# PSUM pools by stage, and a token shift evicted by ScalarE, in a hybrid decoder step

## The chip, the cores and the metric

The kernel runs on one core of one Trainium2 chip. The metric is the device time of one launch in microseconds. Each timed run executes the whole program; the profile is one further execution, recorded by the hardware profiler. TensorE's clock has two levels, 1.2 and 2.4 GHz; the profile gives the granted clock as a share of the upper one.

## The reference, cut to what matters

One layer of a decoder step. 1024 prompt tokens and 8 x 4 sample tokens (1056 in all, model width 1024) go through a norm, one wide projection `w_in`, two parallel branches (a causal convolution and an RWKV-7 recurrence) with gates, and a gated MLP. The change is about the token shift at the head of the recurrent branch:

```python
zr32 = zr.astype(f32)
prev = jnp.concatenate([shift_buf.astype(f32)[:, None, :], zr32[:, :-1]], axis=1)
new_shift = zr[:, -1]
xs = zr32 + (prev - zr32) * rw_mu.astype(f32)
```

So each shifted column is `(1 - mu) * z[t] + mu * z[t-1]`; the first token of the prompt has no predecessor (zero), and the first of each sample sequence has the one in `state_shift`. `zr` has 3360 columns: k, r and v with 1024 each, and 288 for the low-rank inputs of the decay, the in-context rate and the gate. The last row of each sequence is an output (`new_shift`).

## The kernel before

Activations stand with the channel on the partitions and the 1056 tokens along the free dimension, in three blocks of 352. Every projection is made in three fp32r matmuls per 128 channels (high by high, high by low, low by high part), so a tile of 128 output channels is 3 blocks x 8 x 3 = 72 matmuls. `wjob` (line 41) loads a weight tile, makes its high part on ScalarE (L48) and its low part on GpSimd (L49).

The stages are in order:

- `load_in` and `norm_in` (lines 207 to 249): load 9 token tiles and the parameters, transpose the parameters through PSUM (`turn`, copy out in L179), normalise, transpose the tokens (L244) and split them into `hH` and `hL` (L247, L248).
- `mixer_a`, the first mixer stage: four convolution tiles (`conv_proj`), three tiles of low-rank inputs (`lora_in`), and k, r and v of the first two of eight channel groups (`rkv_tile`). `weave` issues, between the matmuls of these tiles, the 30 taps of each convolution (L359, on VectorE) and the low-rank output projections (`lora_out`, evicted by ScalarE in L597, L602 and L609).
- `mixer_b`, the second mixer stage: the recurrence in 16 parts, each prepared (`prep`), staged (`stage`), combined and run through a serial chain of small matmuls (`chain`). `drive` issues these streams by a planned clock, and fills the time between with independent projections: the other 18 tiles of k, r, v, then 16 gate tiles (`gate`) and 8 tiles of the convolution's output (`conv_out`, L441). The streams share `T2N` = 12 SBUF tiles of 576 columns; a stream that finds too few of them free waits (`take`). `prep` takes eight, a group norm three, and one of the eight is held until the part's `stage` ends.
- `tail`: merge of the branches, `w_mix_out`, and the MLP.

The framework gives buffers out and orders each engine's queue before the run, by priorities that follow the order of issue; an instruction whose operands and buffer are free may come to stand in its engine's queue ahead of much that was issued before it. Each engine then works its queue strictly in that order.

PSUM has 8 banks. Both mixer stages and the norm stage share one set: 3 banks with tag `mm` for projections (pool `pm`), and in pool `pw` 2 banks with tag `w` and one each with tags `c`, `x` and `y`. The last three belong to `mixer_b` (`x` is the work tile of a triangular inverse in `stage`, filled in L1025 by a copy of `x0`, which GpSimd makes in L646).

Nine tiles of `mixer_a` and 18 of `mixer_b` go through `shifted`. There, per block, ScalarE writes `(1 - mu) * z` out of PSUM (L490); VectorE adds `mu * z` out of PSUM one column further (L486), adds the first column of the block from a copy `bcol` of the block before (L486 again), and copies the block's last column to `bcol` (L496). The last block also holds the samples: a 24-column add and an 8-column add with the loaded state (L486), and two copies of the last rows to `shcol` (L502, L503). The bank is free when VectorE is through with it.

Of the kernel before, what the change touches and what calls it, by code (L numbers as in the profile page):

```python
# [7 lines left out]
F32 = mybir.dt.float32  # L8
F32R = mybir.dt.float32r
I32 = mybir.dt.int32  # L10
AF = mybir.ActivationFunctionType
ALU = mybir.AluOpType
AX = mybir.AxisListType
PSUM = bass.MemoryType.PSUM
# [3 lines left out]
TP = 1024  # L18
NB = 3
BW = 352  # L20
# [5 lines left out]
NSH = 27  # L26
# [5 lines left out]
class Net:  # L32
# [68 lines left out]
    def build(self):  # L101
        with ExitStack() as es:
# [6 lines left out]
            with ExitStack() as e1:  # L109
                self.rp = self.pool(e1, "wraw", 1)  # L110
                with ExitStack() as e:
                    self.pm = self.pool(e1, "pm", 3, space=PSUM)
                    self.pw = self.pool(e1, "pw", 2, space=PSUM)
                    xs, w0 = self.load_in(e)
                    self.norm_in(e, xs)
                with ExitStack() as e:
                    self.t4 = self.pool(e, "t4", 8)
                    self.mixer_a(w0)
                self.mixer_b()
# [132 lines left out]
    def mixer_a(self, w0):  # L252
        nc, a = self.nc, self.a
# [3 lines left out]
        self.shT = self.cp.tile([128, NSH, 8], F32, name="shT")  # L257
        self.bcol = self.cp.tile([128, NSH, 2], F32, name="bcol")
        self.done = set()
# [221 lines left out]
    def shifted(self, w, j, out, m=128):  # L481

        nc = self.nc
        om, mu = self.omu[:m, j:j + 1], self.par["mu"][:m, j:j + 1]
        bc = self.bcol[:m, j]
        add = lambda o, i: nc.vector.scalar_tensor_tensor(out=o, in0=i, scalar=mu, in1=o, op0=ALU.mult, op1=ALU.add)  # L486

        def ev(b, s, ps):
            t0 = b * BW
            nc.scalar.activation(out=out[:m, s], in_=ps, func=AF.Copy, scale=om)  # L490
            n = min(TP - t0, BW)
            add(out[:m, t0 + 1:t0 + n], ps[:, 0:n - 1])
            if b:
                add(out[:m, t0:t0 + 1], bc[:, b - 1:b])
            if n == BW:
                nc.vector.tensor_copy(out=bc[:, b:b + 1], in_=ps[:, n - 1:n])  # L496
            else:
                x = out[:m, TP:T].rearrange("p (b t) -> p b t", t=4)
                z = ps[:, n:BW].rearrange("p (b t) -> p b t", t=4)
                add(x[:, :, 1:4], z[:, :, 0:3])  # L500
                add(x[:, :, 0], self.shT[:m, j])
                nc.vector.tensor_copy(out=self.shcol[:m, j, 0:1], in_=ps[:, n - 1:n])  # L502
                nc.vector.tensor_copy(out=self.shcol[:m, j, 1:9], in_=z[:, :, 3])  # L503
        yield from self.project_g(w, (self.hH, self.hL), 8, ev, m)
# [163 lines left out]

    T2N = 12

# [321 lines left out]
    def stage(self, n):  # L992

        nc = self.nc
        E, BK, PC, nin, v = self.pr[n]
        LQ = self.sg.tile([128, 8, 128], F32, tag="LQ", name="LQ")
        for g in range(2):
            c4 = slice(4 * g, 4 * g + 4)
            for x in range(2):
                p, q = slice(64 * x, 64 * x + 64), slice(64 - 64 * x, 128 - 64 * x)  # L1000
# [22 lines left out]
        X = self.pw.tile([128, 512], F32, tag="x", name="x", bufs=1)[:, 0:256].rearrange("p (a t) -> p a t", t=32)  # L1023
        tm = self.ln.tile([128, 8, 32], F32, tag="tm", name="tm")
        nc.vector.tensor_copy(out=X, in_=self.x0)  # L1025
        for s in range(31):
            a, m = s // 4 + 1, 31 - s
            nc.vector.tensor_tensor(out=tm[:, :a, :m], in0=L[:, s:s + 1, s + 1:32].to_broadcast([128, a, m]),  # L1028
                                    in1=X[:, :a, s:s + 1].to_broadcast([128, a, m]), op=ALU.mult)
            nc.vector.tensor_tensor(out=X[:, :a, s + 1:32], in0=X[:, :a, s + 1:32], in1=tm[:, :a, :m], op=ALU.add)  # L1030
        Xs = self.ln.tile([128, 8, 32], F32, tag="X", name="X")
# [650 lines left out]
```

## Time and profile before

| | us |
|---|---|
| median of three timed runs | 2560.39 |
| lowest and highest | 2559.02, 2569.00 |
| profiled execution | 2538.03 |
| its span, from the first to the last instruction | 2536.3 |
| busy in it: TensorE, VectorE, ScalarE, GpSimd | 2367.6, 1427.9, 918.7, 909.1 |
| mean granted clock of TensorE | 0.926 |

Times inside the profile are counted from the start of the span. The mixer's first stage runs from about 62 to 340 us, the second from 340 to 1470 us, the tail from there to the end; a window of the profile adds up what every engine did in such a stretch. PE is TensorE, PEld its weight loads, DVE VectorE, ACT ScalarE, POOL GpSimd, SP the engine that issues most DMAs; a q behind the name is the engine's queue. Matmuls overlap each other, so that a busy TensorE can still have gaps that the busy time does not show.

### The profile page before, as it was taken

Reading aid. Unit: us, or ns where it says so; the run is one execution under the profiler, and the core shown is the slowest. Engines: PE = TensorE matmul, PEld = TensorE weight load, DVE = VectorE, ACT = ScalarE, POOL = GpSimd, SP = SyncE. Lnnn points to the kernel's source line nnn. Section 1 sums busy time; section 2 is a strip of 40 time slices with the busy share of each in tenths; the row PEclk is TensorE's granted clock in tenths of the full one; section 3 lists DMA queues with packets and bytes.
Section 4 is the critical chain, followed back from the end, with each engine's and each line's share of the span. In section 5 each row is a group of like instructions: output and inputs, shape, how many; then the busy total and the mean of one; then the engine's idle time right before and its main releaser. Section 6 shows DMA issues by size and latency. Waiting matters only on the chain.

```text
span 2536.3 us, 41660 instructions
## 1 busy us (share of the span) xinstructions
PE 2367.6 (93%) x16094; PEld 2140.9 (84%) x16094; DVE 1427.9 (56%) x3588; ACT 918.7 (36%) x1748; POOL 909.1 (36%) x879
## 2 busy tenths in 40 slices
PE   5889989999788799999989999999999999999998
PEld 4878888777676677777777899999999999999998
DVE  5799955586646674555464434465444534445345
ACT  4133433354244354454434322333222222223125
POOL 3332253244324443443333243433323323323333
PEclk9899987898688698999779999999999999999999
DMA  3223443243233333533323854431111111111111
GB/s 104 56 60 130 171 149 89 81 121 93 78 89 79 93 107 83 140 98 94 94 64 96 273 178 131 128 128 44 44 47 48 44 51 44 47 48 41 54 46 75
DMA packets 307640, 230.64 MB, mean 91 GB/s; under 512 B 90492, under 2 KB 287123, under 8 KB 306921
## 3 DMA queue, kind: packets, MB, share of 16 engines
q1 hardware_dynamic: 307185, 227.80, 31.1%
q8 instruction: 127, 2.08, 0.4%
q14 instruction: 72, 0.59, 0.1%
q0 software_dynamic: 256, 0.17, 0.0%
HBM read 157.45 MB, written 70.45 MB: 90 GB/s over the span
## 4 chain that ended last, share of the span: by engine, by line
PE 66%; DVE 7%; DMA 7%; POOL 3%; issue 2%; ACT 1%; SPq 1%; POOLq 0%; DVEq 0%; ACTq 0%
PE mm L54 52%; PE w L54 7%; DMA L<-dL 4%; PE c L54 2%; PE y L54 2%; PE w L61 2%; DVE tm L1028 1%; DVE x L1030 1%; DVE t L961 1%; DMA ga<-d_ga 0%; POOL BK L982 0%; POOL wlo L49 0%; POOL LQ L1011 0%; DVE lnQ L666 0%; DVE v L486 0%
## 5 line engine op out<-in xcount | busy, mean ns | idle before, releaser
L54 PE MATMUL mm<-hH,whi 128*128 128x352 f32 (+1 forms) x2568 | 887.6, 346 | 27.0 <-DVE bcol L496 11.2
L54 PE MATMUL mm<-hL,whi 128*128 128x352 f32 (+1 forms) x2568 | 866.2, 337 | 0.2 <-DVE hL L248 0.2
L54 PE MATMUL mm<-hH,wlo 128*128 128x352 f32 (+1 forms) x2568 | 862.7, 336 | 0.0
L54 PEld LDWEIGHTS mm<-hH,whi 128*128 128x128 f32 (+1 forms) x2568 | 499.4, 194 | 55.9 <-issue 14.1
L54 PEld LDWEIGHTS mm<-hL,whi 128*128 128x128 f32 (+1 forms) x2568 | 500.9, 195 | 11.2 <-DVE hL L248 0.5
L54 PEld LDWEIGHTS mm<-hH,wlo 128*128 128x128 f32 (+1 forms) x2568 | 500.6, 195 | 8.7 <-issue 0.2
L49 POOL TENSOR_TENSOR wlo<-wraw,whi 128x1024 fp32r<-128x1024 f32 (+2 forms) x123 | 292.5, 2378 | 462.0 <-ACT whi L48 427.9
L48 ACT ACTIVATE whi<-wraw 128x1024 fp32r<-128x1024 f32 (+2 forms) x123 | 126.0, 1025 | 366.8 <-PE mm L54 270.1
L1544 DVE SCALAR_TENSOR_TENSOR c<-u,par,c 128x1024 f32<-128x1024 f32 x96 | 167.0, 1739 | 55.6 <-ACT c L1540 55.6
L359 DVE SCALAR_TENSOR_TENSOR sg<-cu,par,sg 128x1024 f32<-128x1024 f32 x120 | 185.1, 1550 | 3.4 <-ACT sg L357 1.7
L1514 DVE TENSOR_TENSOR u<-mm,rs 128x352 f32<-128x352 f32 x144 | 73.2, 509 | 186.5 <-PE mm L54 186.3
L54 PE MATMUL mm<-fH,whi 128*128 128x352 f32 x504 | 163.4, 324 | 0.0
L1569 DVE TENSOR_TENSOR acc<-mm,acc 128x352 f32<-128x352 f32 x168 | 86.8, 523 | 135.0 <-PE mm L54 135.0
L54 PE MATMUL mm<-fH,wlo 128*128 128x352 f32 x504 | 162.7, 323 | 0.0
L54 PE MATMUL mm<-fL,whi 128*128 128x352 f32 x504 | 162.7, 323 | 0.0
L1028 DVE TENSOR_TENSOR tm<-L,x 128x60 f32<-128x60 f32 (+24 forms) x496 | 99.4, 200 | 79.7 <-DMA L<-dL 72.5
L1030 DVE TENSOR_TENSOR x<-x,tm 128x60 f32<-128x60 f32 (+24 forms) x496 | 105.0, 212 | 7.0
L1525 POOL COPY lr<-u 128x2 f32<-128x2 f32 x48 | 9.0, 187 | 276.3 <-DVE u L1514 267.6
L54 PE MATMUL w<-E,BK 64*128 64x128 f32 x512 | 90.7, 337 | 8.8 <-DVE tm L1028 3.4
L1011 POOL TENSOR_SCALAR_AFFINE_SELECT LQ<-LQ 64x512 f32<-64x512 f32 x64 | 44.1, 690 | 148.3 <-ACT LQ L1007 146.8
L54 PEld LDWEIGHTS mm<-fH,whi 128*128 128x128 f32 x504 | 94.8, 188 | 0.5
L54 PEld LDWEIGHTS mm<-fH,wlo 128*128 128x128 f32 x504 | 95.0, 188 | 0.0
(379 smaller groups left out, 3971.2 us busy)
## 6 DMA issues: line engine op xcount, KB each, us to landing
wraw<-w_in SPq DMA_DIRECT2D x50, 512.0 KB
wraw<-w_up SPq DMA_DIRECT2D x48, 512.0 KB
wraw<-w_down SPq DMA_DIRECT2D x32, 384.0 KB
L<-dL SPq DMA_DIRECT2D x16, 512.0 KB
d_alr<-la SPq DMA_DIRECT2D x8, 528.0 KB
d_cum<-lc SPq DMA_DIRECT2D x8, 528.0 KB
d_gout<-lg SPq DMA_DIRECT2D x8, 528.0 KB
d_k<-k SPq DMA_DIRECT2D x8, 528.0 KB
```

What stands on the lines that cost most here:

```text
L48: nc.scalar.activation(out=hi[:, :nk, :m], in_=raw[:, :nk, :m], func=AF.Copy)
L49: (lo_eng or nc.gpsimd).tensor_tensor(out=lo[:, :nk, :m], in0=raw[:, :nk, :m], in1=hi[:, :nk, :m].bitcast(F32), op=ALU.subtract)
L54: self.nc.tensor.matmul(out, l, r, start=start, stop=stop)
L61: self.nc.tensor.transpose(out, x, ident)
L359: nc.vector.scalar_tensor_tensor(out=c[:, 0:TP], in0=u[:, t:t + TP], scalar=self.col("conv_w", t * 4 + i), in1=c[:, 0:TP], op0=ALU.mult, o ...
L961: nc.vector.scalar_tensor_tensor(out=t1[:, u], in0=r[:, u], scalar=self.col("r_k", 2 * J + u), in1=km[:, u], op0=ALU.mult, op1=ALU.mult)
L1011: nc.gpsimd.affine_select(out=w, in_=w, pattern=[[0, 4], [1, 2], [1, 64]], compare_op=ALU.is_ge, fill=0.0, base=-1, channel_multiplier=-1)
L1028: nc.vector.tensor_tensor(out=tm[:, :a, :m], in0=L[:, s:s + 1, s + 1:32].to_broadcast([128, a, m]), in1=X[:, :a, s:s + 1].to_broadcast([12 ...
L1030: nc.vector.tensor_tensor(out=X[:, :a, s + 1:32], in0=X[:, :a, s + 1:32], in1=tm[:, :a, :m], op=ALU.add)
L1514: nc.vector.tensor_tensor(out=u[:, 2 + t0:2 + t0 + m], in0=p, in1=rs[:, t0:t0 + m], op=ALU.mult)
L1544: nc.vector.scalar_tensor_tensor(out=c[:, 0:TP], in0=u[:, t:t + TP], scalar=wt, in1=c[:, 0:TP], op0=ALU.mult, op1=ALU.add)
L1569: nc.vector.tensor_tensor(out=acc[i][:, s], in0=ps[:, :BW], in1=acc[i][:, s], op=ALU.add)
```

## The change

The norm stage and the first mixer stage get PSUM pools of their own, 5 banks with tag `mm` and 3 with tag `w`; the set with 3, 2 and the tags `c`, `x`, `y` is opened after them, for `mixer_b`. In `shifted`, ScalarE reads the bank twice: once for `(1 - mu) * z`, once for `mu * z` into a new SBUF pool `shift` of two tiles; it also copies the last rows to `shcol`. VectorE adds that tile one column further, as one add of 352 columns that reaches into the next block's first column, and so is issued when the next block has been evicted. `bcol`, its copies and its one-column adds go. To make room in SBUF, `T2N` becomes 11, and the product tile `tm` of the triangular inverse shrinks to 96 columns.

```diff
             with ExitStack() as e1:
                 self.rp = self.pool(e1, "wraw", 1)
-                with ExitStack() as e:
-                    self.pm = self.pool(e1, "pm", 3, space=PSUM)
-                    self.pw = self.pool(e1, "pw", 2, space=PSUM)
-                    xs, w0 = self.load_in(e)
-                    self.norm_in(e, xs)
-                with ExitStack() as e:
-                    self.t4 = self.pool(e, "t4", 8)
-                    self.mixer_a(w0)
+                with ExitStack() as ep:
+                    self.pm = self.pool(ep, "pm", 5, space=PSUM)
+                    self.pw = self.pool(ep, "pw", 3, space=PSUM)
+                    with ExitStack() as e:
+                        xs, w0 = self.load_in(e)
+                        self.norm_in(e, xs)
+                    self.shp = self.pool(e1, "shift", 2)
+                    with ExitStack() as e:
+                        self.t4 = self.pool(e, "t4", 8)
+                        self.mixer_a(w0)
+                self.pm = self.pool(e1, "pmb", 3, space=PSUM)
+                self.pw = self.pool(e1, "pwb", 2, space=PSUM)
                 self.mixer_b()
...
-        self.bcol = self.cp.tile([128, NSH, 2], F32, name="bcol")
...
-        bc = self.bcol[:m, j]
-        add = lambda o, i: nc.vector.scalar_tensor_tensor(out=o, in0=i, scalar=mu, in1=o, op0=ALU.mult, op1=ALU.add)
+        held = []
+
+        def add():
+            t0, n, z = held.pop()
+            nc.vector.tensor_tensor(out=out[:m, t0 + 1:t0 + 1 + n], in0=out[:m, t0 + 1:t0 + 1 + n], in1=z[:m, :n], op=ALU.add)
 
         def ev(b, s, ps):
             t0 = b * BW
+            n = min(TP - t0, BW)
             nc.scalar.activation(out=out[:m, s], in_=ps, func=AF.Copy, scale=om)
-            n = min(TP - t0, BW)
-            add(out[:m, t0 + 1:t0 + n], ps[:, 0:n - 1])
-            if b:
-                add(out[:m, t0:t0 + 1], bc[:, b - 1:b])
+            z = self.shp.tile([128, BW], F32, tag="z", name="z")
+            nc.scalar.activation(out=z[:m], in_=ps, func=AF.Copy, scale=mu)
+            if n < BW:
+                nc.scalar.copy(out=self.shcol[:m, j, 0:1], in_=ps[:, n - 1:n])
+                nc.scalar.copy(out=self.shcol[:m, j, 1:9], in_=ps[:, n:BW].rearrange("p (b t) -> p b t", t=4)[:, :, 3])
+            if held:
+                add()
             if n == BW:
-                nc.vector.tensor_copy(out=bc[:, b:b + 1], in_=ps[:, n - 1:n])
+                held.append((t0, n, z))
             else:
+                held.append((t0, n - 1, z))
+                add()
                 x = out[:m, TP:T].rearrange("p (b t) -> p b t", t=4)
-                z = ps[:, n:BW].rearrange("p (b t) -> p b t", t=4)
-                add(x[:, :, 1:4], z[:, :, 0:3])
-                add(x[:, :, 0], self.shT[:m, j])
-                nc.vector.tensor_copy(out=self.shcol[:m, j, 0:1], in_=ps[:, n - 1:n])
-                nc.vector.tensor_copy(out=self.shcol[:m, j, 1:9], in_=z[:, :, 3])
+                nc.vector.tensor_tensor(out=x[:, :, 1:4], in0=x[:, :, 1:4],
+                                        in1=z[:m, n:BW].rearrange("p (b t) -> p b t", t=4)[:, :, 0:3], op=ALU.add)
+                nc.vector.scalar_tensor_tensor(out=x[:, :, 0], in0=self.shT[:m, j], scalar=mu, in1=x[:, :, 0], op0=ALU.mult, op1=ALU.add)
...
-    T2N = 12
+    T2N = 11
...
-        tm = self.ln.tile([128, 8, 32], F32, tag="tm", name="tm")
+        tmf = self.ln.tile([128, 96], F32, tag="tm", name="tm")
...
-            nc.vector.tensor_tensor(out=tm[:, :a, :m], in0=L[:, s:s + 1, s + 1:32].to_broadcast([128, a, m]),
+            tm = tmf[:, :a * m].rearrange("p (a t) -> p a t", t=m)
+            nc.vector.tensor_tensor(out=tm, in0=L[:, s:s + 1, s + 1:32].to_broadcast([128, a, m]),
```

## Rows read from the trace of the kernel before

**Rows 1.** The page, part 1: busy us, share of the span, instructions.

```profile
PE 2367.6 (93%) x16094; PEld 2140.9 (84%) x16094; DVE 1427.9 (56%) x3588; ACT 918.7 (36%) x1748; POOL 909.1 (36%) x879
```

**Rows 2.** Windows: PE, PEld, DVE, ACT, POOL busy us (count), clock, DMA share, GB/s.

```profile
0.00:62.00 62.00, 33.84 (x176) 25.84 (x177) 34.48 (x107) 28.94 (x50) 19.40 (x47) 0.93 0.32 102
...
98.00:163.00 65.00, 52.92 (x289) 45.09 (x288) 64.80 (x70) 21.92 (x34) 31.89 (x18) 0.89 0.20 54
163.00:310.00 147.00, 142.50 (x763) 124.17 (x762) 145.54 (x144) 57.67 (x104) 37.17 (x22) 0.98 0.38 133
310.00:340.00 30.00, 30.00 (x188) 29.61 (x187) 12.56 (x26) 7.22 (x13) 5.67 (x8) 1.00 0.44 148
340.00:1470.00 1130.00, 1015.56 (x7899) 842.62 (x7899) 659.20 (x2418) 492.71 (x1096) 438.48 (x453) 0.85 0.40 108
1470.00:2536.00 1066.00, 1058.33 (x6592) 1039.70 (x6590) 492.86 (x812) 303.72 (x443) 367.85 (x329) 1.00 0.23 68
```

**Rows 3.** Timeline of 10 to 25 us: start, us, engine, line [idle before, releaser].

```profile
10.58 2.26 SPq L203 DMA_DIRECT2D xt<-x_prompt  x5
...
11.68 0.41 PE L177 MATMUL w<-ident,st 107*128 107x107 f32 x1 [11.68 <-DMA st<-norm_final_g]
...
12.84 2.08 DVE L235 TENSOR_SCALAR xt<-xt,ry 128x1024 f32<-128x1024 f32 x3
...
22.51 0.43 DVE L1025 COPY x<-x 128x256 f32<-128x256 f32 x1 [7.59 <-POOL x L646]
22.84 0.26 DVE L179 COPY par<-w 128x107 f32<-128x107 f32 x1
```

**Rows 4.** Waits of TensorE, 60 to 340 us: total us, times, longest.

```profile
PE mm L54 <- DVE bcol L496: 8.6, 4, 4.4
PE w L372 <- ACT ls L597: 2.1, 1, 2.1
...
PE mm L54 <- ACT sg L337: 0.6, 1, 0.6
```

**Rows 5.** Windows of line 486 alone, 100 to 335 us: VectorE busy.

```profile
100.00:335.00 235.00, 27.41 (x63) 0.96 0.33 113
```

**Rows 6.** VectorE's groups by shape, 340 to 940 us: count, busy us, mean ns, idle.

```profile
L932 DVE TENSOR_TENSOR kn<-kn,alr 128x512 f32<-128x512 f32 x8 | 5.6, 699 | 0.1
```

**Rows 7.** VectorE's groups by shape, 62 to 340 us.

```profile
L359 DVE SCALAR_TENSOR_TENSOR sg<-cu,par,sg 128x1024 f32<-128x1024 f32 x120 | 185.1, 1550 | 3.4 <-ACT sg L357 1.7
...
L486 DVE SCALAR_TENSOR_TENSOR r<-bcol,par,r 128x1 f32<-128x1 f32 x4 | 3.8, 952 | 0.0
...
L496 DVE COPY bcol<-mm 128x1 f32<-128x1 f32 x16 | 2.4, 147 | 0.0
...
L486 DVE SCALAR_TENSOR_TENSOR r<-mm,par,r 128x351 f32<-128x351 f32 x4 | 2.3, 568 | 0.0
...
L486 DVE SCALAR_TENSOR_TENSOR lx<-bcol,par,lx 128x1 f32<-128x1 f32 x4 | 1.5, 368 | 0.0
...
L486 DVE SCALAR_TENSOR_TENSOR lx<-bcol,par,lx 32x1 f32<-32x1 f32 x2 | 0.4, 202 | 0.0
```

**Rows 8.** Timeline of VectorE, 300 to 335 us.

```profile
307.54 3.60 DVE L359 SCALAR_TENSOR_TENSOR sg<-cu,par,sg 128x1024 f32<-128x1024 f32 x2
...
330.95 0.55 DVE L486 SCALAR_TENSOR_TENSOR v<-mm,par,v 128x319 f32<-128x319 f32 x1 [3.87 <-ACT v L490]
```

**Rows 9.** ScalarE's groups by shape, 62 to 340 us.

```profile
L490 ACT ACTIVATE r<-mm,omu 128x352 f32<-128x352 f32 x6 | 3.3, 550 | 1.3 <-PE mm L54 1.1
```

**Rows 10.** Waits of TensorE, 335 to 940 us.

```profile
PE mm L54 <- DVE shcol L503: 8.6, 2, 6.5
```

**Rows 11.** Timeline of TensorE where the tail's pools begin.

```profile
1469.36 0.40 PE L54 MATMUL mm<-hH,whi 128*128 128x352 f32 x1 [0.41 <-ACT whi L48]
```

**Rows 12.** Lines 1126 and 441: count, min/median/max ns, first and last start.

```profile
L1126 DVE COPY R<-c x64: 276/292/295, 428.8 to 1394.2; 128x128 f32<-128x128 f32 x64
...
L441 DVE SCALAR_TENSOR_TENSOR ga<-ga,mm x24: 509/521/522, 1416.9 to 1468.7; 128x352 f32<-128x352 f32 x24
```

More of the change, by code (lines that the diff above doesn't have):

```diff
@@ L1027, in stage @@
             a, m = s // 4 + 1, 31 - s
-            nc.vector.tensor_tensor(out=tm[:, :a, :m], in0=L[:, s:s + 1, s + 1:32].to_broadcast([128, a, m]),
+            tm = tmf[:, :a * m].rearrange("p (a t) -> p a t", t=m)
+            nc.vector.tensor_tensor(out=tm, in0=L[:, s:s + 1, s + 1:32].to_broadcast([128, a, m]),
                                     in1=X[:, :a, s:s + 1].to_broadcast([128, a, m]), op=ALU.mult)
-            nc.vector.tensor_tensor(out=X[:, :a, s + 1:32], in0=X[:, :a, s + 1:32], in1=tm[:, :a, :m], op=ALU.add)
+            nc.vector.tensor_tensor(out=X[:, :a, s + 1:32], in0=X[:, :a, s + 1:32], in1=tm, op=ALU.add)
         Xs = self.ln.tile([128, 8, 32], F32, tag="X", name="X")
```

## The prediction

> **What bounds the kernel now.** I read the page first, then busy time by stage, then who waited for whom in each stage, then single rows. TensorE is the engine to look at: it is busy 93% of the span [rows 1]. The stage table [rows 2] says where it is not. From 1470 us on it is busy 1058 of 1066 us at clock 1.00, and the change touches nothing there. From 0 to 62 us (load and norm) it is busy for 34 of 62 us. From 98 to 163 us it loses 12 of 65 us while VectorE is busy 64.80 of 65. From 163 to 310 us VectorE is still busy 145.54 of 147 us, now with TensorE at 142.50. From 310 to 340 us TensorE runs without a gap and VectorE is mostly idle. So the first mixer stage (62 to 340 us) is paced by VectorE until about 310 us, and its end by TensorE. Then come 1130 us of second mixer stage with TensorE busy 1016 us at a mean clock of 0.85.
>
> Two things in the early part matter here. In the norm stage VectorE stands idle for 7.59 us in front of the copy of L1025, until GpSimd has made the tile `x0` in L646. That copy belongs to the second mixer stage. It stands in VectorE's queue at 22.51 us only because its PSUM bank (tag `x`, in the pool `pw`) is free from the start. Behind it stands the parameter copy of L179: its transpose ended on TensorE at 12.09 us (11.68 + 0.41), but it ran at 22.84 [rows 3]. All activations with those parameters wait for it. In the first mixer stage TensorE's waits name the evictions: 8.6 us for the one-column copy L496, 2.1 for an evicted bank of the `w` tag, and seven more groups down to 0.6, together 18.6 us [rows 4]. With five banks and ScalarE alone to free them, most of these lose their cause; what is late next is the question.
>
> **The change, part by part.** *The early copy.* The tag `x` now lives in `pwb`, which opens when the first pools have closed, at the end of the first mixer stage. So the copy of L1025 can't stand at 22.51 us any more. The parameter copy then runs when VectorE ends its three scalings at 14.92 us (12.84 + 2.08), 7.9 us earlier. The inputs don't hold it back: the last prompt tiles are issued by 12.84 us [rows 3], and from 23 us on that stage computes. The copy itself (0.43 us) moves to the second mixer stage. I take -7.6, between -10 (a third bank for the transposes helps too) and -4 (the loads late instead).
>
> *VectorE's work in the first mixer stage.* Nine tiles are shifted there (three of the low-rank inputs, six of k, r, v). Their line L486 costs 27.41 us [rows 5]; the copies L496, L502 and L503 are 36 of 0.15 us, 5.3 more. What goes per tile is three adds out of PSUM of 0.57 us, two one-column adds, four small copies and a 24-column add. What comes is three adds of 352 columns with both operands in SBUF and one of 24 columns; the 8-column add (about 2.5 us for nine) stays. Such a 352-column add is not in the trace. The nearest row, two SBUF operands at 512 columns, has a mean of 0.699 us [rows 6], so by columns 0.48 us undisturbed. But one-column adds with SBUF operands take 0.20 us at best, 0.95 in their worst group and 0.57 in the mean of 16 (four groups, the worst and the mildest shown), while the PSUM adds keep to 0.57 us with 351 columns; the mean of the 120 taps, 1.55 us, is inflated as well [rows 7]. So an SBUF add pays 0 to 0.75 us, in the mean 0.37, for what else goes on. Removed: 27.41 + 5.3 - 2.5 = 30.2 us. Added, undisturbed: 27 x 0.48 + 9 x 0.23 = 15.0 us; at the worst 27 x 1.23 + 9 x 0.98 = 42.0; at the mean 27 x 0.85 + 9 x 0.60 = 28.4. The bounds are thus -15 and +12 us, the middle -2; I take -3, since the adds that stand where no weight split runs pay nothing.
>
> The Trainium skill has a rule that speaks against this part: by "SBUF — State Buffer", section "Who interferes with whom", a VectorE instruction with two SBUF inputs contends with a GpSimd instruction that reads SBUF, and one with a single SBUF input does not. The one-column adds against the PSUM adds [rows 7] bear it out: 0.95 us against 0.57 us for 351 times the columns. By the rule all 27 adds enter that contention; if each met it as the worst group did, the sum would be 12 us longer instead of 3 shorter. That is rival B.
>
> *TensorE's lead.* VectorE paces the stage until its last taps end at 311.1 us (307.54 + 3.60); the stage's last block is evicted at 330.95 [rows 8]. This tail of 20 us shrinks if TensorE is further ahead by then. Two more banks allow it; but ScalarE works in order: from the third block on, a `z` buffer comes free only by a VectorE add, behind that wait stand the evictions of the low-rank outputs and the weight splits, and TensorE waits for those with three `w` banks instead of two. I take -5, a quarter of the tail, between 0 and -18.6 (all of TensorE's waits). The added ScalarE work is three activations of 0.55 us a tile [rows 9] and two copies of 1 and 8 columns, which by that row can't be over 0.3 us each: 2.2 us a tile, 20 us for nine, in a stage where ScalarE is busy 21.92 of 65 and 57.67 of 147 us [rows 2]. Its own idle time hides it; without that cover it would be those 20 us.
>
> *The second mixer stage.* 18 more tiles. TensorE waits there 8.6 us for L503, in two waits [rows 10]; those evictions now leave VectorE's queue. Against that stands the new wait of ScalarE for VectorE's add before it may fill `z`, with the chain's scalings queued behind it. I take -2, from -9 to +9 (the same size the other way). The pools change hands between the stages; where that happens today, at 1469 us, TensorE goes from one set to the other with 0.41 us of idle, and that for a weight split [rows 11]. I take 0.
>
> *Eleven `T2` tiles for twelve.* A preparation takes eight, a group norm three, and a stage holds one; so these three no longer fit together. The chain's last step starts at 1394.2 us, the stage's last filler is evicted at 1468.7 [rows 12], so a chain that ends some us later still finds cover in 74 us of independent matmuls. I take +2, from 0 to +27 (rival C). The contiguous `tm` costs nothing that I can name: the same elements by as many instructions.
>
> **Sum.** -7.6 - 3 - 5 - 2 + 2 = -15.6 us on the profiled execution of 2538.0 us (span 2536.3): 2522.4, a ratio of 0.9939. The three timed runs have a median of 2560.4, 0.9% above that execution; I apply the ratio to it: 2544.7 us.
>
> **Rivals.** *A: TensorE is set free.* All 18.6 us of waits go, because VectorE keeps up (adds undisturbed). With the 7.6 us, the -2 and +2, and the lost clock back (0.89 over 65 us, 7 us, [rows 2]) that is -33: 2527 us. For it: the waits named are mostly for banks. Against: VectorE is busy 99% up to 310 us.
>
> *B: the adds stay dear.* VectorE's share grows by 12 us instead of shrinking, and takes back the early gain: -7.6 - 5 - 2 + 2 + 12 is 0, and with half of the 12 it is -6.6: 2554 to 2560, I name 2556. For it: 0.95 us for one column, and the rule above. Against: only one group of four is that slow.
>
> *C: slower.* Place: the second mixer stage. With eleven tiles a preparation or a group norm waits for a tile to come back, its small matmuls stand in TensorE's queue in front of the fillers, and TensorE idles and shows a lower clock more often. The clock is 0.85 over 1130 us [rows 2]; each 0.01 less costs 1130 x 0.01 / 0.85 = 13 us. At 0.83 it is +27 against -15.6: 2572 us. The point from which it decides is a clock lower by 0.012, which eats the gain. For it: this stage is the one full of waits. Against: the 74 us of cover.
>
> *D: the front of VectorE's queue stays blocked*, by another instruction of a later stage: then the first 7.6 us stay, and the sum is -8: 2552. For it: L1025 shows that such instructions come early. Against: none other stands there now.
>
> **Chances.** Forecast 0.48, A 0.15, B 0.17, C 0.13, D 0.07. About 0.5% (12.8 us) is what a measurement of this kernel can tell from no change. Of the forecast's 0.48 I count 0.37 beyond that bound and 0.11 within; A is faster; B and D are within; of C 0.11 is slower and 0.02 within. So faster 0.52, same 0.37, slower 0.11. The range that leaves out no more than 2 in 10 runs from 2522 (just under A) to 2566 (part of C); the forecast's own is 2532 to 2556.
>
> **What would show it.** Right: VectorE has no wait for GpSimd's `x0`, and L179 runs near 15 us; the taps start some 7 us earlier; TensorE waits for no copy of L496 or L502 in the first mixer stage; the last taps end near 300 and that stage's last eviction near 315 us; ScalarE shows waits for the adds at the `z` activation. A mean of the adds of 0.5 to 0.95 us is the forecast, above 1.1 is B. Wrong: L179 still near 22 us (D), a mean clock under 0.84 in the second mixer stage (C), or TensorE's waits gone without the first mixer stage ending earlier, which would mean that VectorE's sum is larger than I think.

## The result, and the profile after

The kernel after takes 2594.2 us (median of four runs, 2587.7 to 2605.5) against 2563.6 for the kernel before (four runs): ratio 1.0144, 95% interval 1.0106 to 1.0181. The prediction said 2544.7, and 2522 to 2566 as its range: wrong in size and in sign. The ratios leave out executions that are more than 1.5% above the fastest of their kernel, the medians don't, and a ratio is not the quotient of two medians (here 1.0119, inside the interval).

Executions of one kernel differ by about 1% to either side, and each profile is one of them. The profile of before is one of its fastest executions (2538.0 us; 34 later runs lie between 2537 and 2589), that of after is a middle one (2593.8 us), so the two profiles differ by 56 us where the medians differ by 31.

The page's part 1 of the kernel after:

```profile
PE 2410.9 (93%) x16094; PEld 2168.0 (84%) x16094; DVE 1424.4 (55%) x3426; ACT 958.9 (37%) x1883; POOL 920.8 (36%) x879
```

TensorE is busy for 43 us more than in [rows 1], with the same instructions. The windows say where (after; columns as in [rows 2]):

```profile
0.00:62.00 62.00, 41.98 (x238) 36.16 (x239) 34.80 (x108) 29.54 (x52) 19.45 (x47) 0.92 0.40 126
98.00:163.00 65.00, 49.33 (x283) 44.42 (x281) 64.67 (x53) 26.30 (x48) 32.21 (x15) 0.87 0.19 57
163.00:310.00 147.00, 142.45 (x762) 122.80 (x761) 139.91 (x114) 65.53 (x134) 43.42 (x25) 0.99 0.40 144
...
340.00:1470.00 1130.00, 1006.30 (x7559) 814.68 (x7559) 629.75 (x2268) 498.53 (x1151) 419.04 (x439) 0.81 0.34 94
1470.00:2536.00 1066.00, 1061.57 (x6564) 1042.95 (x6565) 480.66 (x763) 284.90 (x403) 361.35 (x317) 1.00 0.25 76
```

In the first 62 us TensorE does more than before. Between 340 and 1470 us it gets 340 matmuls less done, at a clock of 0.81 against 0.85. The early part answers to [rows 3, 4, 7, 8]. First the timeline of VectorE, 10 to 25 us:

```profile
12.92 2.08 DVE L239 TENSOR_SCALAR xt<-xt,ry 128x1024 f32<-128x1024 f32 x3
14.91 0.26 DVE L183 COPY par<-w 128x107 f32<-128x107 f32 x1
```

The parameter copy runs at 14.91 us instead of 22.84, right behind the scalings. Waits of TensorE in the first mixer stage of after (46 to 325 us: total, times, longest):

```profile
PE mm L54 <- ACT whi L48: 9.2, 1, 9.2
PE mm L54 <- POOL wlo L49: 6.5, 2, 4.9
PE mm L54 <- ACT shcol L504: 2.0, 1, 2.0
```

No eviction of VectorE is among them; the weight splits are late instead. VectorE's groups by shape in the same stretch (count, busy us, mean ns, idle), and its last add of that stage:

```profile
L362 DVE SCALAR_TENSOR_TENSOR sg<-cu,par,sg 128x1024 f32<-128x1024 f32 x120 | 182.0, 1534 | 3.5 <-ACT sg L360 1.7
...
L493 DVE TENSOR_TENSOR k<-k,z 128x352 f32<-128x352 f32 x4 | 4.9, 1219 | 0.0
...
L493 DVE TENSOR_TENSOR v<-v,z 128x352 f32<-128x352 f32 x4 | 3.9, 984 | 7.9 <-ACT v L499 7.9
L493 DVE TENSOR_TENSOR r<-r,z 128x352 f32<-128x352 f32 x4 | 3.9, 981 | 3.9 <-ACT r L499 3.9
L493 DVE TENSOR_TENSOR lx<-lx,z 128x352 f32<-128x352 f32 x4 | 3.5, 867 | 0.0
...
319.51 0.48 DVE L493 TENSOR_TENSOR v<-v,z 128x319 f32<-128x319 f32 x1
```

An add of 352 columns with two SBUF operands takes 0.87 to 1.22 us in the mean of a group where the one out of PSUM took 0.57 [rows 7]. These means mix two sorts. Ten of the sixteen adds of 128 x 352 take 0.50 to 0.60 us. The other six take 1.17 to 2.70 us, and each of them ends 0.38 us after a GpSimd instruction that was running when it began, as here (a free add, then GpSimd's weight split and an add that meets it):

```profile
301.29 0.50 DVE L493 TENSOR_TENSOR r<-r,z 128x352 f32<-128x352 f32 x1
305.25 2.40 POOL L49 TENSOR_TENSOR wlo<-wraw,whi 128x1024 fp32r<-128x1024 f32 x1 [1.75 <-ACT whi L48]
305.64 2.39 DVE L493 TENSOR_TENSOR r<-r,z 128x352 f32<-128x352 f32 x1 [3.86 <-ACT r L499]
```

So such an add isn't slower by a factor; it lasts until the GpSimd instruction has ended. That doesn't happen beside every one: an add beside the making of `l_wal` took 0.51 us.

ScalarE waits for these adds in front of `z`, and the weight splits stand behind it in its queue. Its longest such wait is this one:

```profile
129.58 0.56 ACT L501 ACTIVATE z<-mm,par 128x352 f32<-128x352 f32 x1 [7.32 <-DVE lx L493]
```

TensorE's 9.2 us for `whi` end at 150.2 us. ScalarE starts that split at 149.09 us, and at 144.41 in e9 (below), where VectorE still adds out of PSUM. Ahead of it stands GpSimd's `l_rh`, 5.88 us long here and 3.58 there, and ahead of that the split of its input on ScalarE, at 141.99 us here and 139.60 there.

The stage's last add starts 11.4 us earlier than in [rows 8].

The chain and the stage's end (after; answers to [rows 12]):

```profile
L1139 DVE COPY R<-c x64: 272/292/292, 422.2 to 1456.2; 128x128 f32<-128x128 f32 x64
L444 DVE SCALAR_TENSOR_TENSOR ga<-ga,mm x24: 511/520/523, 1474.6 to 1524.6; 128x352 f32<-128x352 f32 x24
```

The chain (first to last copy of R) starts 6.6 us earlier and lasts 1034.0 us instead of 965.4. The convolution's output tiles begin when it is over: their first eviction comes 18.4 us after the last copy, against 22.7 before. They need the space of the stage's buffers (`fillers` calls `conv_in`, which closes that pool, only when the chain's last part is done), so none of them can stand beside the chain.

From the last add of the first mixer stage to that first eviction it is 1155 us against 1086 (319.51 to 1474.6, 330.95 to 1416.9). Windows over these stretches, after and then before:

```profile
320.00:1475.00 1155.00, 1027.06 (x7670) 834.86 (x7669) 641.85 (x2286) 511.75 (x1176) 426.05 (x446) 0.81 0.34 96
```

```profile
331.00:1417.00 1086.00, 976.90 (x7673) 805.29 (x7672) 640.74 (x2393) 479.13 (x1082) 428.33 (x446) 0.85 0.37 99
```

The same 7670 matmuls: TensorE is busy 50 us longer on them at the lower clock (1027 is 1.051 times 977; 0.85 is 1.049 times 0.81), and idle 19 us longer. In this pair of profiles the first stage gave 11 us, the second took 69.

### The profile page after: what moved, and what is told of

Read it like the earlier page. It is cut to its first block, busy times and chain, and to the rows that moved or that the text cites. A ratio compares the mean times of both kernels' runs of the same rounds, so it can differ in the third digit from the quotient of the medians.

```text
span 2592.0 us, 41662 instructions
## 1 busy us (share of the span) xinstructions
PE 2410.9 (93%) x16094; PEld 2168.0 (84%) x16094; DVE 1424.4 (55%) x3426; ACT 958.9 (37%) x1883; POOL 920.8 (36%) x879
## 4 chain that ended last, share of the span: by engine, by line
PE 68%; DVE 7%; DMA 6%; issue 2%; POOL 2%; ACT 1%; SPq 1%; POOLq 0%; ACTq 0%; DVEq 0%
PE mm L54 52%; PE w L54 7%; DMA L<-dL 4%; PE y L54 3%; PE c L54 3%; PE w L61 2%; DVE x L1043 1%; DVE tm L1041 1%; DVE t L973 1%; DMA d_ma<-ga 1%; DMA ga<-d_ga 0%; DVE k L493 0%; POOL y L1207 0%; POOL alr L969 0%; PE w L1436 0%
## 5 line engine op out<-in xcount | busy, mean ns | idle before, releaser
L1557 DVE SCALAR_TENSOR_TENSOR c<-u,par,c 128x1024 f32<-128x1024 f32 x96 | 167.1, 1740 | 55.6 <-ACT c L1553 55.6
L1118 ACT ACTIVATE SP<-UV,PC 64x64 f32<-64x64 f32 x192 | 63.6, 342 | 88.8 <-DVE UV L1158 80.2
L54 PEld LDWEIGHTS w<-E,BK 64*128 64x128 f32 x512 | 76.4, 222 | 22.7 <-issue 13.0
```

What stands on the lines that cost most here:

```text
L54: self.nc.tensor.matmul(out, l, r, start=start, stop=stop)
L1118: nc.scalar.activation(out=at(SP, u, x), in_=src(x)[:, u], func=AF.Copy, scale=PC[hs[x], 4 * u + c:4 * u + c + 1])
L1557: nc.vector.scalar_tensor_tensor(out=c[:, 0:TP], in0=u[:, t:t + TP], scalar=wt, in1=c[:, 0:TP], op0=ALU.mult, op1=ALU.add)
```

## The experiments

All ran beside the kernel before. In the table "tiles" is `T2N`; "ScalarE" says in which mixer stage it makes the shift; "chain" is from the first to the last copy of R; "last fillers" are the independent matmuls that TensorE's order has beside the chain's last two parts, and those left when it ends (counted in the traces, which lack some records, so good to about ten). The profiles behind the columns are single executions: that of e5 was its fastest (2572.8 us), that of e9 its slowest (2546.4).

| run | tiles | ScalarE | ratio (95%) | chain us | last fillers |
|---|---|---|---|---|---|
| before | 12 | none | 1 | 965 | 159, 78; 98 |
| after | 11 | both | 1.0144 (1.0106 to 1.0181) | 1034 | 29, 0; 0 |
| e1 | 11 | none, old pools | 1.0093 (1.0060 to 1.0126) | 1008 | 95, 75; 0 |
| e2 | 12 | first | 0.9998 (0.9962 to 1.0034) | 975 | 152, 75; 95 |
| e3 | 11 | first | 1.0043 (1.0008 to 1.0078) | 1025 | 100, 42; 0 |
| e4 | 12 | both | 0.9972 (0.9932 to 1.0012) | 975 | 151, 70; 49 |
| e5 | 11 | both | 1.0120 (1.0037 to 1.0203) | 1011 | 100, 48; 0 |
| e6 | 11 + own gol | both | 1.0005 (0.9967 to 1.0043) | 986 | 181, 111; 11 |
| e7 | 10 | both | 1.0176 (1.0104 to 1.0248) | 1037 | 0, 0; 0 |
| e8 | 12 | none | 0.9888 (0.9824 to 0.9952) | 981 | 158, 78; 89 |
| e9 | 12 | none | 0.9884 (0.9842 to 0.9927) | 981 | 158, 78; 95 |
| e10 | 12 | first | 0.9979 (0.9943 to 1.0015) | 994 | 152, 75; 92 |
| e11 | 13, X over L | none | 1.0061 (1.0030 to 1.0092) | 1009 | 0, 0; 0 |
| e12 | 12 | second | 0.9889 (0.9840 to 0.9938) | 974 | 151, 70; 49 |
| e17 | 12, X over L | none | 0.9947 (0.9909 to 0.9984) | 986 | 0, 0; 0 |

**Tiles or ScalarE (e1 to e4).** e1 is the kernel before with one number changed:

```diff
-    T2N = 12
+    T2N = 11
```

> The kernel before with one number changed: eleven T2 tiles for twelve. In the profiles the first stages end about 14 us earlier after the change and the second mixer stage lasts about 68 us longer; the medians differ by 31 us, so by them the second stage costs about 45 us. Theory T2: the eleven tiles are that whole cost, because a preparation (eight tiles) and a group norm (three) no longer fit beside a stage (one): then this kernel has none of the early gain and all of the loss, 2564 + 45 = 2609 us, and the mean granted clock from 340 us on falls from 0.85 to about 0.81. Rival S: ScalarE's evictions of the 18 tiles in the second mixer stage (three activations and a wait for VectorE's add per block) are the cost: then this kernel takes 2564 us, within 5. Rival O: the order that results from any shift of the fillers is the cost: then it is anything from -10 to +40 and the kernels of this call don't add up.

Measured 2577.8 against 2560.6 us, ratio 1.0093: eleven tiles cost something by themselves, but 17 to 24 us and not 45. The chain grew by 42 us.

e2 and e3 keep the new `shifted` for the first mixer stage only; in the second the old one comes back:

```diff
-        yield from self.shifted(self.wjob(...), jj, t)
+        f = self.shifted if self.early else self.shifted_b   # shifted_b: adds out of PSUM, bcol
+        yield from f(self.wjob(...), jj, t)
```

> The kernel after, with its PSUM pools and ScalarE's shift in the first mixer stage, but the shift of the kernel before (adds out of PSUM) in the second one, and twelve T2 tiles. T2 and S agree: only the early gain is left, 14 us measured in the profiles: 2564 - 14 = 2550 us, and the chain from its first step (about 425 us) to its last group norm lasts the 969 us of before. Rival O: the second mixer stage, started 14 us earlier, comes out in another order and loses part of this again: 2555 to 2590 us, with the chain longer than 990 us.

Measured 2557.3, ratio 0.9998. The chain is near that of before (975 us), as both theories said, but the early gain isn't in the time. Something else was eating it.

> As the kernel with ScalarE's shift in the first mixer stage alone, but with eleven T2 tiles; it differs from the kernel after only in who shifts the 18 tiles of the second mixer stage. Theory T2: no better than the kernel after, 2594 us within 6, chain near 1035 us. Rival S: 2550 us as with twelve, chain near 969 us. Half and half would be 2572.

Measured 2568.6, ratio 1.0043: near half and half, so neither theory alone.

e4 is the kernel after with `T2N = 12` and one `z` buffer in the second stage; in both stages the add of a block now stands ahead of the next `z`.

> The kernel after with twelve T2 tiles; the room for the twelfth comes from z, which has one buffer in the second mixer stage instead of two (so there the add of the block before is issued ahead of the next z). Theory T2: the loss is gone and the early gain stays: 2550 us, chain near 969 us. Rival S: 2594 us or more (one z buffer makes ScalarE wait longer for VectorE's add), chain 1035 us or longer.

Measured 2546.6, ratio 0.9972, chain 975 us. ScalarE's shift is in both stages and the loss is gone: theory S falls.

**What about the tiles (e5 to e7).** e5 and e7 are e4 with `T2N = 11` and 10. In e6, with eleven, the group norm takes two tiles (in every fourth part still three), and its third has a buffer of its own:

```diff
-            ld.append(self.T2([128, 2, 256], x))
+            ld.append(self.T2([128, 2, 256], x) if x == "bvl" else self.ln.tile([128, 2, 256], F32, tag="gol", name="gol"))
...
-            yield from self.take(3, 1)
+            g = 3 if n % 4 == 3 else 2
+            yield from self.take(g, 1)
```

> The kernel with ScalarE's shift in both mixer stages and one z buffer in the second (2546.6 us with twelve T2 tiles), now with eleven; from the kernel after it differs only in the z buffers of the second stage (one for two). So far eleven tiles cost 17 us in the kernel before (2577.8 against 2560.6) and 11 us with ScalarE's shift in the first stage alone (2568.6 against 2557.3), but 48 us between the kernel after (2594.2) and the one with twelve tiles and one z buffer. Theory T2: the tiles are the cost here too, and z is not: 2580 to 2596 us, second mixer stage (from the last block of the first to the eviction of the first conv tile) near 1150 us against 1086. Rival Z: the second z buffer is what costs, since two let ScalarE run ahead of the chain's scalings; then this kernel loses only the 11 to 17 us of the tiles: 2557 to 2566 us, stage near 1105 us.

Measured 2612.8 (six runs, 2572.8 to 2630.3; before 2565.3), ratio 1.0120 (1.0037 to 1.0203), which rests on three of them (2572.8, 2588.2 and 2609.9): near the kernel after (1.0144), so the second `z` buffer is not the main cause. The interval is too wide to say that it costs nothing.

> ScalarE's shift in both stages, one z buffer, eleven T2 tiles, but the group norm takes two of them instead of three: its tile gol has a buffer of its own (2 KB, about what the twelfth T2 tile took). A preparation (8), a group norm (2) and a stage (1) again add up to eleven. Theory G: what costs with eleven is that these three don't fit together; then this kernel is back at the level of twelve, 2547 us within 8, stage near 1086 us. Rival R: any pool of eleven costs, because a tile then comes round one allocation earlier and its first writer waits for the last reader; then it stays near the other kernel of eleven tiles, within 8 us of it.

Measured 2558.7 on the same chip, ratio 1.0005 (0.9967 to 1.0043), just inside e4's interval. That is 1.2% under e5 by the ratios (30 us between the medians of the executions that they take, 2558.2 and 2588.2; 54 us between those of all), and the interval lies clear of the kernel after's. It is still a pool of eleven; what changed is what the group norm takes from it. So theory G holds against R as R was put: a preparation (8), a group norm (3) and a stage (1) have to fit together. With `gol` apart there are again twelve buffers in all, so the run doesn't tell the sum of what is held from the mere number of buffers. Nor does it tell whether the missing tile acts by waits in the run or by the order of issue, which `take` also sets.

> ScalarE's shift in both stages, one z buffer, ten T2 tiles. With ten, a preparation (8) and a group norm (3) exclude each other altogether; with eleven they exclude each other only while a stage holds its tile. Theory G: the step from eleven to ten is at least as dear as that from twelve to eleven: 2600 us or more, mean granted clock of the second mixer stage 0.79 or lower. Rival F (the loss is one threshold at twelve, and below it the order of the fillers decides): within 10 us of the kernel with eleven.

Measured 2612.2, ratio 1.0176 (1.0104 to 1.0248), chain 1037 us. By the medians of all executions that is e5's time, by the ratios somewhat more; the intervals overlap, so whether the tenth tile costs as much again isn't settled.

How a late tile looks: the loads of the preparation of part 8. The queue of SP in the kernel after, 847 to 866 us (start, us, line, what is moved):

```profile
847.94 0.52 SPq L1212 DMA_DIRECT2D d_y<-y  x1
...
850.67 0.58 SPq L905 DMA_DIRECT2D k<-d_k  x1
860.03 0.52 SPq L419 DMA_DIRECT2D d_cs<-lnC  x1
860.60 0.64 SPq L905 DMA_DIRECT2D cum<-d_cum  x1
861.87 1.75 SPq L1326 DMA_DIRECT2D d_y<-y1s  x4
863.67 0.57 SPq L905 DMA_DIRECT2D alr<-d_alr  x1
...
864.94 0.61 SPq L905 DMA_DIRECT2D v<-d_v  x1
```

and in e9 (twelve tiles):

```profile
782.22 0.56 SPq L896 DMA_DIRECT2D k<-d_k  x1
782.88 0.58 SPq L896 DMA_DIRECT2D cum<-d_cum  x1
783.56 0.56 SPq L896 DMA_DIRECT2D alr<-d_alr  x1
784.21 0.56 SPq L896 DMA_DIRECT2D r<-d_r  x1
786.33 1.19 SPq L896 DMA_DIRECT2D v<-d_v  x1
```

In e9 the loads are issued within 4 us. In the kernel after they take 14 us and alternate with stores of tiles of the same pool: `y` of a group norm, `lnC`, `y1s`. Each is followed by one or more loads. But e6 has this late preparation too (its last load is issued 61 us after the end of part 5, against 59 in the kernel after and 19 in e9) without its loss, so this one place is not the whole of it.

**The pools alone (e8, e9).** e8 is the kernel before with only the pools' part of the change; e9 adds the contiguous `tm`.

> The kernel before with the PSUM pools of the kernel after (five dense and three shared banks in the first stages, three and two with c, x and y from the second mixer stage on), the shift with its adds out of PSUM everywhere, twelve T2 tiles. It separates the pools from ScalarE's shift in the first stages. Theory V (VectorE paces the first mixer stage): the pools give the 7.6 us of the early copy (parameter copy at 15 us, norm's end at 47 instead of 55.6) and nothing else: taps end at 302 us, last block of that stage evicted at 331 instead of 339. Rival B5 (five banks are what shortens it): taps end near 294 and the last block near 325, as with ScalarE's shift. Either way the time is 2552 to 2560 us.

Measured 2537.0 (before 2565.3), ratio 0.9888 (0.9824 to 0.9952): the fastest form so far. The last taps start at 299.6 us, the block that I had counted at 339 us is evicted at 326, and VectorE's last add of the stage starts at 316.8 us (after: 319.5; before: 330.95). The last add is this row:

```profile
316.82 0.55 DVE L489 SCALAR_TENSOR_TENSOR v<-mm,par,v 128x319 f32<-128x319 f32 x1 [4.59 <-ACT v L493]
```

So the pools (the early copy and the banks) give all of the early gain, ScalarE's shift none of it. Theory V falls, and the time came out below what either theory said: the stage ends 14 us earlier, the whole kernel gains some 29, and where the rest is gained isn't shown.

> The pools alone (2537.0 us, ratio 0.989) with the contiguous tm of the kernel after; twelve T2 tiles, adds out of PSUM everywhere. The instructions on tm take 220 ns (60 columns) in both forms of it. Theory N: tm costs nothing, ratio 0.989 again, within 0.005. Rival M: tm is the difference between the pools alone (0.989) and the kernel with ScalarE's shift in the first stage and the contiguous tm (1.000); then this one is near 1.000.

Measured 2536.3, ratio 0.9884: `tm` costs nothing that these intervals show.

**ScalarE's shift, stage by stage (e10, e12).** e10 is e2 with the old `tm`; e12 is e4 with the old `shifted` in the first stage (`f = self.shifted_b if self.early else self.shifted`). Both ran on one chip with e9.

> The pools and ScalarE's shift in the first mixer stage alone, twelve T2 tiles, tm as in the kernel before. Against the pools alone it adds only ScalarE's shift of the first stage. In the profiles so far both reach the last block of that stage at the same time (326 and 325 us). Theory N: the shift in the first stage is worth nothing, ratio 0.985 to 0.993 like the pools alone. Rival H: it costs (it goes together with a ratio of 1.000 so far): 0.997 to 1.003.

> The pools, ScalarE's shift in the second mixer stage alone (one z buffer, contiguous tm), twelve T2 tiles. Theory N: ScalarE's shift neither helps nor hurts with twelve tiles, ratio 0.985 to 0.995. Rival S2: taking the 18 tiles' evictions off VectorE's queue helps the chain: 0.975 to 0.985. Rival S3: ScalarE's wait for the adds holds the chain's scalings up: 0.997 or more.

Measured 2561.7 (0.9979) for the first stage, 2539.7 (0.9889) for the second. With twelve tiles ScalarE's shift costs nothing in the second stage and some 24 us in the first (0.96% by e10 over e9; 0.8% by e4 over e12, 1.2% by e2 over e9), the other way round than I had looked for it. With twelve tiles, three kernels with it there stand at 0.9972 to 0.9998, three without at 0.9884 to 0.9889. Part of it is seen: VectorE's last add of the stage starts at 323.8 us in e10 and 323.5 in e4, at 316.8, 315.3 and 314.0 in e8, e9 and e12. With it goes TensorE's wait for `whi`, near 150 us: 9.2, 9.0, 8.9 and 9.7 us in the kernel after, e2, e4 and e10, with the shift on ScalarE there, and none in e8, e9 and e12. The other 15 us or so stay open: the order of the second stage differs between e10 and e9, but hardly between e4 and e12.

**Thirteen tiles (e11, e17).** Room for a thirteenth came from copying X over L:

```diff
-    T2N = 12
+    T2N = 13
...
-        Xs = self.ln.tile([128, 8, 32], F32, tag="X", name="X")
+        Xs = L[:, 0:8]
```

> The pools alone with thirteen T2 tiles (the room comes from the contiguous tm and from the copy of X, which takes the place of L, read for the last time before). Theory G (a preparation of 8, a group norm of 3 and a stage of 1 have to fit together) puts the threshold at twelve: thirteen gives no more than 10 us, ratio 0.985 to 0.992. Rival L (each tile counts): another 15 to 45 us off, ratio 0.972 to 0.983.

Measured 2580.0, ratio 1.0061: slower than twelve, which neither theory had. Two things had been changed at once; e17 has the copy over L alone.

> The pools alone with the contiguous tm and twelve T2 tiles (2536.3 us, ratio 0.988), with one thing changed: the copy of X out of PSUM goes to the first columns of L instead of to a tile of its own, so the next load of L waits until X has been stored. Theory A (this wait, not the thirteenth tile, made the kernel with thirteen tiles slow): ratio 1.003 or more; in TensorE's order the last two parts of the chain have no filler here either. Rival L13 (the thirteenth tile did it): 0.985 to 0.992.

Measured 2541.4, ratio 0.9947 (0.9909 to 0.9984), between the two. So the copy over L costs about 0.6% (the intervals of e9 and e17 overlap) and the thirteenth tile another 1.1%. More tiles are not simply better; why the thirteenth hurts isn't settled. In e11 the last gate is evicted at 1295 us, 135 us before the chain's last copy of R.

**The fillers (e13 to e16).** In most of the slower kernels TensorE runs out of fillers before the chain ends. e13 and e14 hold the last three gates back; the first is the kernel after, the second e11:

```diff
+    HOLD = {15: 14, 14: 13, 13: 12}
...
+        if after is not None:          # one column of the state that part n left
+            nc.vector.tensor_copy(out=raw[:, 0, 0:1], in_=after)
         nc.sync.dma_start(out=raw[:, :nk, :m], in_=src.rearrange("(k p) c -> p k c", p=128))
```

> The kernel after, eleven T2 tiles, with one thing changed: the weight loads of the last three gates wait for chain parts 12, 13 and 14 (a one-column copy of the carried state into the weight buffer ahead of each load). TensorE's order is the same up to part 12; from there the parts have 94, 72, 54 and 90 filler matmuls beside them instead of 102, 179, 29 and 0. Theory F (the loss is the stretch at the chain's end in which TensorE has no filler): 216 matmuls of 0.158 us (379 in the 60 us from 1470 us on) are 34 us of work that moves into idle time: 2560 to 2570 us for 2594, and the granted clock from 1300 us to the chain's end rises from about 0.66 to 0.8 or more. Rival T2 (the chain itself is held up by the missing tile, fillers or not): no gain, 2588 us or more, since the idle time only moves ahead.

> The pools alone with thirteen T2 tiles and X copied over L (2580.0 us), with the last three gates held in the same way: the last four parts of the chain have 84, 72, 56 and 88 filler matmuls beside them instead of 209, 91, 0 and 0. Theory F: 34 us of work moves into idle time: 2540 to 2552 us, ratio 0.992 to 0.998. Rival T2: 2575 us or more.

Measured 2597.4 (1.0154) and 2596.2 (1.0174): no gain in the first (1.0144 without), a loss in the second (1.0061 without). Theory F falls. e17 speaks against it too: no filler beside its last two parts, and still faster than before.

e15 and e16 add a fourth product to every gate, 384 matmuls, in the kernel after and in e9:

```diff
+                if four:
+                    self.mm(ps[:m, :BW], wl[:, k, :m], xl[:, k, s], k == 0, False)
```

> The kernel after with a fourth product (low part by low part) in each gate: 384 more filler matmuls, at 0.158 us (379 in 60 us) 61 us more work for TensorE. In its order the last parts then have 127, 120, 178 and 148 fillers beside them instead of 166 to 0, and 102 are left when the chain ends. Theory F: most of that work falls into time in which TensorE had nothing: 2594 to 2620 us, less than half of the 61 us. Rival W: it is paid in full, 2655 us.

> The pools alone with the contiguous tm (2536.3 us, twelve tiles, some 90 fillers left at the chain's end) with the same fourth product in each gate. Here the fillers don't run out, so both theories have the work paid in full: 2536 + 61 = 2597 us, 2585 to 2605. If it costs less than 40 us, extra filler work is cheap in any kernel, and the run on the kernel after tells nothing.

Measured 2596.0 (1.0178) and 2622.0 (1.0263). In the kernel after the added work costs 2 us by the medians and 9 by the ratios, in e9 86 and 97, where I had expected 61 in e9. The 0.158 us a matmul behind that 61 were taken at a clock of 1.00; at e9's 0.83 (340 to 1470 us) the sum is 73 us, an estimate. Here is the end of the chain, first in the kernel after, then in e15 (windows, and the copies of R):

```profile
1325.00:1425.00 100.00, 76.13 (x625) 55.67 (x624) 63.39 (x236) 45.52 (x103) 32.97 (x32) 0.69 0.30 93
1425.00:1525.00 100.00, 80.66 (x542) 68.60 (x542) 32.51 (x76) 28.50 (x51) 23.77 (x19) 0.79 0.57 172
```

```profile
1325.00:1425.00 100.00, 97.12 (x742) 81.08 (x743) 48.68 (x209) 34.61 (x81) 28.79 (x27) 0.85 0.27 75
1425.00:1525.00 100.00, 91.79 (x654) 81.99 (x655) 37.18 (x76) 37.40 (x64) 22.40 (x18) 0.98 0.64 212
...
L1141 DVE COPY R<-c x64: 273/292/294, 428.9 to 1450.2; 128x128 f32<-128x128 f32 x64
```

With more matmuls in these 200 us, TensorE's clock rises from 0.69 to 0.85 and from 0.79 to 0.98, and the chain still ends at 1450.2 us (1456.2 without). So with eleven tiles the chain and what feeds it set the end of the second mixer stage, and TensorE has room for 384 matmuls there. The same work in e9 moves what comes behind it. The copies of R and the convolution's tiles, in e9 and then in e16:

```profile
L1130 DVE COPY R<-c x64: 273/291/293, 421.8 to 1402.6; 128x128 f32<-128x128 f32 x64
L444 DVE SCALAR_TENSOR_TENSOR ga<-ga,mm x24: 512/520/522, 1425.6 to 1476.9; 128x352 f32<-128x352 f32 x24
```

```profile
L1132 DVE COPY R<-c x64: 272/291/293, 423.2 to 1415.6; 128x128 f32<-128x128 f32 x64
L446 DVE SCALAR_TENSOR_TENSOR ga<-ga,mm x24: 513/520/522, 1499.3 to 1552.3; 128x352 f32<-128x352 f32 x24
```

The chain ends 13 us later and the convolution's first tile comes 73.7 us later: in e9 TensorE sets the end.

**What is settled, and what not.** Three parts were measured: the pools -30 us (ratio 0.9884), ScalarE's shift in the first stage +24 (e10 over e9: 1.0096), and eleven tiles, at +38 (e5 over e4: 1.0148), +24 (e1) and +12 (e3 over e2). With the first of the three, 0.9884 x 1.0096 x 1.0148 is 1.0127, and the kernel after has 1.0144; with the other two it is 1.0072 and 1.0024. So that the parts add up is not shown: either the missing tile costs more the more of the change is there, or the spread of e5 hides the difference. What is shown is the sign of each: the pools gain, the other two lose (the tile by e1 and by e5 over e4; the intervals of e2 and e3 overlap). Not settled: through which of the sixteen parts the missing tile works and whether by waits or by order, and most of what the shift costs in the first stage. The best kernels are e8, e9 and e12, at 0.9884 to 0.9889 of the time before.

## Why the prediction was wrong

*The early copy:* right. Forecast 14.92 us for the parameter copy, measured 14.91; the norm stage ends 9.3 us earlier (55.6 to 46.3 us, last split of tokens), where I took 7.6 and 10 as the far end.

*VectorE's work:* the sum was right, its worth wrong. The new adds cost 21.92 + 3.70 + 2.01 = 27.6 us (windows on their three lines) against 27.4 [rows 5] + 5.3 us for the old lines: 5.1 us less, forecast 3. With 352 columns they take 1.01 us in the mean (of 128 x 352), between the 0.95 that I called the forecast and the 1.1 of rival B; over all 27 adds it is 0.82. By the Trainium skill ("SBUF — State Buffer", section "Who interferes with whom"), a VectorE instruction with two SBUF inputs contends with a GpSimd instruction that reads SBUF. The trace agrees: 1.17 to 2.70 us for the six adds that end with a GpSimd instruction, 0.50 to 0.60 for the other ten. But the pools alone, with the adds out of PSUM, end the stage earlier still (316.8 us, after 319.5), and in the whole kernel the shift costs some 24 us there (e10 over e9). This is the second step that failed: the -3 was right as a sum of VectorE's work and said nothing of what waits for the adds.

*TensorE's lead:* -5 was about right for the banks and wrong for the change. In e8, e9 and e12 the last add comes 14.1, 15.6 and 17.0 us earlier, 6 to 7 us more than the end of the norm stage; in the kernel after it comes 11.4 us earlier, 2 us more than that. The waits for `bcol` went, but in e8 one of 6.4 us for it remains, and the gain is larger. So the gain is that of the pools, and the hazard that I had named under this heading, weight splits late behind ScalarE's wait for `z`, took part of it back.

*The second mixer stage:* -2 forecast; e12 against e9 shows none (0.9889 and 0.9884). The wait for `z` that I had feared costs nothing there.

*Eleven tiles:* this step failed. I took +2, since "a chain that ends some us later still finds cover in 74 us of independent matmuls". Only the first 23 us of those 74 are gates; the rest is the convolution's output, which can't begin before the chain has ended, so it is no cover; [rows 12] showed it, its first start being 22.7 us after the chain's last one. The chain itself has no slack when tiles are short: 384 more matmuls fit beside it, and three gates held back to its last parts change nothing. The term was +12 to +38 us by the three pairs above, and why it differs between them stays open.

*Rival C* was the right place, at a chance of 0.13. I put the clock at 0.83 and it fell to 0.81; my price, 13 us per 0.01, makes 52 us of that, and the stage lost 50 us in busy time and 19 in idle. But the clock isn't what sets the end: e15 has 0.86 between 340 and 1470 us and the same end. Nor does the clock simply follow TensorE's busy share in a stretch: between 425 and 525 us of the kernel after it is 0.71 with TensorE busy 99 of 100 us. What makes it fall in the slower kernels isn't shown.

## What to carry to other kernels

A buffer count that is cut to make room is a change of its own: add up what has to be held at once (here 8 + 3 + 1), and time the cut alone before pricing the rest. Work is cover only if nothing on the path has to end before it can begin, so look up what its buffers and inputs wait for. To see whether a serial chain or an engine sets a stage's end, add independent work: what costs 2 to 9 us in one kernel and 86 to 97 in the other tells the two apart. And before moving an engine's operand from PSUM to SBUF, look in the trace for what the other engines run beside it.

## What the hardware showed

Span times mean granted clock is nearly one number for all kernels with the same work: 2342 to 2361 us in the mean of each kernel's runs (e17: 2334), whether the time is 2536 or 2612 us; with the 384 matmuls it is 2409 and 2406. So a longer time comes with a lower mean clock (0.925 for e9, 0.908 for the kernel after), and two executions of one kernel differ in the same way: e8 took 2511 us at 0.934 and 2546 us at 0.921. Which of the two brings the other isn't shown by this product.
